# Round 1's first head of a hybrid trunk: two seven-product quads run product by product in turn

## The chip, the cores and the metric

The kernel runs on one core of one Trainium2 chip. Its engines are PE (TensorE), DVE (VectorE), ACT (ScalarE), POOL (GpSimd) and SP (SyncE, which issues nearly all DMAs). The metric is the time of one execution in microseconds (us), as the median of several runs. Times inside an execution are read from a profile of one of them.

## What is computed

One layer of a decoder trunk over 2048 tokens of width 1024, in fp32. Cut to what matters:

```python
hn = rms_norm(h, norm_g)
proj = jnp.einsum('bld,de->ble', hn, w_in)            # 1024 -> 8 * 512
cx, cb, cc, cg, q, k, v, rg = jnp.split(proj, 8, axis=-1)
conv_out = short_conv(cx, cb, cc) * silu(cg)
qf, kf = rotary(q, pos) * 128 ** -0.5, rotary(k, pos)
ret = head_group_norm(retention_chunkwise(qf, kf, v)) # 4 heads of 128, chunks of 128
mixed = concatenate([conv_out, ret * silu(rg)])
out = rms_norm(h + einsum('ble,ed->bld', mixed, w_out))
```

Nearly all matmul work is the projection by `w_in` and the one by `w_out`.

## The kernel before, in words

**Rounds, units, quads.** The tokens are done in two rounds of 1024. In each, four conv groups and four retention heads ("units") are run in a fixed order; each unit needs two "quads". A quad is a product of a 2 x 2 arrangement of weight blocks (for a head: keys and values by the lower and upper half of the 1024 inputs; then queries and gates) by a 2 x 2 arrangement of input blocks, with 512 tokens in each. It is done in one of two ways.

- `quad_plain` (line 293) multiplies all eight pairs of blocks. Its input operands are the blocks themselves, numbers 0, 1, 7 and 5.
- `quad` (line 236) does the same with seven products, in the Strassen-Winograd manner. Its input operands 0 to 6 are two blocks and five others (sums of blocks, and block 5); its weights are four blocks and three sums, which POOL forms in `stationary`. Three of the seven products are copied out of PSUM by ACT (line 243, `tc`), and DVE adds them to others. `take(i, j, bank, copy)` receives each result.

**Parts.** Every fp32 operand is split into a high part (ACT, line 112, or line 115 where the norm's gain is multiplied in) and a low part (DVE, line 113 or 116), and a product of two blocks is three matmuls (low by high, high by low, high by high) for each of four slices of 128 inputs: 12 matmuls of 128x512. High and low parts of weights are `wh` and `wl`, in rings of three buffers (RING); those of inputs `mh` and `ml`, one buffer for each operand and slice; number 7 has no buffer of its own and uses that of number 4. So an input operand of round 1 can be written once the last quad of round 0 has finished its product of that number.

**Sums.** The four sums of input blocks that round 1 needs are formed during round 0 by DVE (`prepare`), written to DRAM (`sums_x`) and read back by `prepared` (tiles `t`).

**The start of round 1.** `moving` loads the 16 blocks of `x` and splits them (operands 0, 1, 7, 5). Then the weights of the first quad are loaded and split as plain blocks, in buffers of operand 3. Head 0 runs keys and values with `quad_plain`: 96 matmuls. Two of the four sums are loaded and split ahead of it in the program, two behind it (`rest_of_sums`), and behind those the last conv group's result is stored. Queries and gates follow as a seven-product `quad`; in its steps the values and keys are taken to the other layout: `part` copies the 16-bit halves apart on ACT (line 677), a DMA transpose moves them (line 670), and `join` and `join_keys` copy them together again (lines 769 and 760). `weigh` scales the values (line 775). The state and score matmuls (lines 807 to 831) come after.

**Other work on DVE.** Keys and queries are rotated by `rotary`: two half operations (lines 658 and 659), a product and a sum (lines 660 and 661). Gates are multiplied by a row factor (line 750). POOL also does two products for the end of each conv group (line 596).

**The order of the rows.** Every engine takes its instructions in a fixed order. It is set at build time by a scheduler that goes by the program's order and by its own estimate of times; `issue_after` and priorities bend it. Where engines depend on each other, semaphores make them wait, and what is behind a waiting instruction on its engine waits too.

## Time and profile before

| | us |
|---|---|
| median of 3 runs | 869.21 (868.64 to 869.86) |
| the profiled execution's own time | 868.33 |
| its span, first to last instruction | 866.5 |
| PE busy | 855.4 (99%) |
| DVE busy | 725.7 (84%) |
| ACT busy | 497.8 (57%) |
| POOL busy | 394.6 (46%) |

The granted TensorE clock is 0.998 of full speed over the span. Round 1's first plain matmul starts at 360.70 us of the span.

In a timeline, a line gives start (us from the start of the span), duration, engine, line of the kernel, operation, result and operands with their shapes, and how many like it follow each other; in brackets stands the idle time of the engine just before it and what ended it. Operations overlap a little with the one before on their engine, and matmuls by half, so what an operation takes is read from the distance of two starts. In the lines of windows, each engine's busy time is followed by its number of instructions, and at the end stand the granted clock, the DMA engines' busy share and GB/s.

### The profile page before, as it was taken

Reading aid. Unit: us, or ns where it says so; the run is one execution under the profiler, and the core shown is the slowest. Engines: PE = TensorE matmul, PEld = TensorE weight load, DVE = VectorE, ACT = ScalarE, POOL = GpSimd, SP = SyncE. Lnnn points to the kernel's source line nnn. Section 1 sums busy time; section 2 is a strip of 40 time slices with the busy share of each in tenths; the row PEclk is TensorE's granted clock in tenths of the full one; section 3 lists DMA queues with packets and bytes.
Section 4 is the critical chain, followed back from the end, with each engine's and each line's share of the span. In section 5 each row is a group of like instructions: output and inputs, shape, how many; then the busy total and the mean of one; then the engine's idle time right before and its main releaser. Section 6 shows DMA issues by size and latency. Waiting matters only on the chain.

```text
span 866.5 us, 12699 instructions
## 1 busy us (share of the span) xinstructions
PE 855.4 (99%) x4216; PEld 705.1 (81%) x4216; DVE 725.7 (84%) x1194; ACT 497.8 (57%) x899; POOL 394.6 (46%) x286
## 2 busy tenths in 40 slices
PE   9999999999999999999999999999999999999996
PEld 6778888888787778788888888888888888788885
DVE  7899988888988977989789898988767799877663
ACT  8676548384755554948374757544333566545553
POOL 0662332423145554352242323354746555677773
PEclk9999999999999999999999999999999999999999
DMA  9724235454656633845264845646123584555431
GB/s 339 233 79 89 72 85 154 113 149 135 159 169 190 199 98 98 313 149 146 62 158 121 159 134 124 205 113 216 48 78 81 173 326 136 169 165 178 156 134 73
DMA packets 127218, 129.51 MB, mean 149 GB/s; under 512 B 58352, under 2 KB 75568, under 8 KB 127152
## 3 DMA queue, kind: packets, MB, share of 16 engines
q1 hardware_dynamic: 126576, 128.30, 50.0%
q8 instruction: 33, 0.54, 0.3%
q10 hardware_dynamic: 576, 0.40, 0.1%
q14 instruction: 33, 0.27, 0.1%
HBM read 90.91 MB, written 25.17 MB: 134 GB/s over the span
## 4 chain that ended last, share of the span: by engine, by line
PE 78%; DVE 6%; issue 1%; ACT 0%; POOL 0%; POOLq 0%; DVEq 0%
PE pj L236 66%; PE pj L293 5%; PE ms L831 1%; PE ms L820 1%; PE ms L830 1%; PE ms L807 1%; DVE wl L113 1%; PE ms L456 1%; DVE ml L113 1%; DVE ml L116 0%; DVE yo L121 0%; DVE yo L906 0%; DVE yo L941 0%; ACT n L407 0%; DVE tc L121 0%
## 5 line engine op out<-in xcount | busy, mean ns | idle before, releaser
L236 PE MATMUL pj<-mh,wl 128*128 128x512 f32 x1008 | 396.0, 393 | 1.3 <-DVE wl L113 0.7
L236 PE MATMUL pj<-mh,wh 128*128 128x512 f32 x1008 | 393.1, 390 | 0.0
L236 PE MATMUL pj<-ml,wh 128*128 128x512 f32 x1008 | 392.9, 390 | 0.0
L112 ACT CAST wh<-ra 128x512 fp32r<-128x512 f32 x216 | 133.9, 620 | 232.1 <-PE pj L236 193.6
L236 PEld LDWEIGHTS pj<-mh,wl 128*128 128x128 f32 x1008 | 189.3, 188 | 43.1 <-issue 1.5
L113 DVE TENSOR_TENSOR wl<-ra,wh 128x512 fp32r<-128x512 f32 x216 | 192.4, 893 | 36.6 <-ACT wh L112 35.2
L236 PEld LDWEIGHTS pj<-mh,wh 128*128 128x128 f32 x1008 | 189.3, 188 | 39.4
L236 PEld LDWEIGHTS pj<-ml,wh 128*128 128x128 f32 x1008 | 189.3, 188 | 38.1
L121 POOL TENSOR_TENSOR sa<-ra 128x512 f32<-128x512 f32 x36 | 54.1, 1504 | 108.8 <-DMA ra<-in_w_in 50.5
L124 POOL TENSOR_TENSOR ra<-sa,ra 128x512 f32<-128x512 f32 x36 | 51.3, 1424 | 81.8 <-DVE wl L113 79.6
L124 POOL TENSOR_TENSOR ra<-ra 128x512 f32<-128x512 f32 x36 | 59.1, 1641 | 59.2 <-PE ms L456 48.9
L151 POOL TENSOR_TENSOR ra<-ra 128x512 f32<-128x512 f32 x36 | 61.5, 1709 | 47.3 <-issue 35.2
L243 ACT COPY tc<-pj 128x512 f32<-128x512 f32 x108 | 62.6, 580 | 0.1
L293 PE MATMUL pj<-mh,mh 128*128 128x512 f32 x128 | 51.0, 401 | 0.6 <-ACT mh L115 0.6
L293 PE MATMUL pj<-mh,ml 128*128 128x512 f32 x128 | 50.0, 390 | 1.0 <-DVE ml L113 1.0
L293 PE MATMUL pj<-ml,mh 128*128 128x512 f32 x128 | 48.0, 391 | 0.0
L843 POOL TENSOR_TENSOR rp<-rs,neg_half 128x4 f32<-128x4 f32 x16 | 19.4, 1211 | 46.4 <-DVE rs L121 46.2
L596 POOL TENSOR_TENSOR c<-c,rr 128x512 f32<-128x512 f32 x14 | 25.7, 1834 | 22.2 <-DVE c L637 14.1
L906 DVE TENSOR_TENSOR yo<-pj,yo 128x512 f32<-128x512 f32 (+1 forms) x33 | 22.0, 671 | 15.9 <-PE pj L236 8.5
L917 POOL TENSOR_TENSOR z<-yo,final_g 128x512 f32<-128x512 f32 x16 | 26.8, 1674 | 18.6 <-DVE yo L906 18.6
L847 DVE TENSOR_SCALAR pm<-ms,mv,rp 128x128 f32<-128x128 f32 x64 | 21.9, 403 | 11.8 <-POOL rp L843 11.8
L112 ACT CAST wh<-sa 128x512 fp32r<-128x512 f32 x36 | 22.2, 618 | 16.0 <-PE pj L236 15.8
(153 smaller groups left out, 1223.2 us busy)
## 6 DMA issues: line engine op xcount, KB each, us to landing
ra<-in_w_in SPq DMA_DIRECT2D x126, 256.0 KB, 2.9
x<-in_xT SPq DMA_DIRECT2D x48, 256.0 KB, 5.0
w<-in_w_out SPq DMA_DIRECT2D x32, 256.0 KB, 4.7
ra<-mixed SPq DMA_DIRECT2D x32, 256.0 KB, 2.7
yo<-in_x SPq DMA_DIRECT2D x32, 256.0 KB, 4.6
ra<-in_x SPq DMA_DIRECT2D x16, 256.0 KB, 3.3
mixed<-c SPq DMA_DIRECT2D x16, 256.0 KB, 2.5
sums_x<-x SPq DMA_DIRECT2D x16, 256.0 KB, 2.8
```

The costliest lines, as they stand in the source:

```text
L112: nc.scalar.copy(out=hi, in_=src)
L113: lowered[0] = eng.tensor_tensor(out=lo, in0=src, in1=hi.bitcast(F32), op=ALU.subtract)
L121: eng.tensor_tensor(out=out, in0=a, in1=b, op=ALU.add)
L124: eng.tensor_tensor(out=out, in0=a, in1=b, op=ALU.subtract)
L151: summed[0] = nc.gpsimd.tensor_tensor(out=a12, in0=a12, in1=a11, op=ALU.subtract)
L236: nc.tensor.matmul(bank, a[:, ks], b, start=first and kt == 0 and n == 0, stop=kt == KH - 1 and n == 2, skip_group_check=not first,)
L243: copied[0] = nc.scalar.copy(out=c, in_=bank)
L293: nc.tensor.matmul(banks[i], a[:, ks], b, start=half + kt + n == 0, stop=half == 1 and kt == KH - 1 and n == 2,)
L596: eng.tensor_tensor(out=out, in0=a, in1=b, op=ALU.mult)
L847: nc.vector.tensor_scalar(out=y[:, cs], in0=o[:, cs], scalar1=mv[:, c, 0:1], scalar2=rp[:, c, :], op0=ALU.subtract, op1=ALU.mult,)
L906: last[0] = nc.vector.tensor_tensor(out=y[:, cs], in0=pp[:, cs], in1=y[:, cs], op=ALU.add)
L917: nc.gpsimd.tensor_tensor(out=ys[i][j], in0=y, in1=final_g[:, j * HB : (j + 1) * HB], op=ALU.mult)
```

## The change

Round 1's head 0 now runs both its quads as seven products, in turn: keys and values' product 0, queries and gates' product 0, keys and values' product 1, and so on. Four new functions replace `moving` and `quad_plain` there.

- `quads` runs the 14 products, with two PSUM banks for each quad, and takes results as `quad` does. Its `between` steps are called after each pair of products.
- `stationary_in_turn` gives a quad's weight parts one at a time, and forms its sums in the four buffers of the blocks themselves, with four POOL operations as before but no fifth buffer.
- `moving_in_turn` splits operands 0 and 1 ahead of the quads; the others follow as steps between the products: sums 2, 3, 4, block operand 5, sum 6.
- Operand 7, and with it four loads of `x` and four splits, is gone in round 1, and so are the four splits of plain weights; the seven splits of `stationary_in_turn` take their place.

In `head`, the keys are now split apart for the transpose after products 3 and 6, the values after products 5 and 6; the joins and weighing come behind the two quads. The store of the last conv group's result moves into the step of sum 6.

```diff
+    def stationary_in_turn(blocks):
+        a11, a12, a21, a22 = blocks
...
+        yield parts(a11)
+        add(nc.gpsimd, a21, a21, a22)
+        sub(nc.gpsimd, a11, a21, a11)
+        yield parts(a12)
+        sub(nc.gpsimd, a12, a12, a11)
+        yield parts(a11)
+        yield parts(a21)
+        sub(nc.gpsimd, a21, a22, a11)
+        yield parts(a21)
+        yield parts(a12)
+        yield parts(a22)
...
+        blocks(0, 0)
+        blocks(1, 0)
+        steps = [
+            lambda: sums(m, 1), lambda: sums(m, 0), lambda: sums(m, 2), lambda: blocks(1, 1), lambda: sums(m, 3),
+        ]
...
+    def quads(ws, m, takes, between=()):
...
+        for i in range(7):
+            for n, take in enumerate(takes):
+                if i < 2:
+                    banks[n][i] = ps_proj()
+                bank = banks[n][1 if i in (1, 3, 5) else 0]
+                product(n, i, bank, i in (0, 1, 3))
...
+            next(between, idle)()
...
-        quad(stationary(load_raw(w_loads(2 * h + 1))), m, take, (split_late, middle, late_middle))
-        with tc.issue_after(copied[0].ins):
+        if len(first) > 0:
+            steps = list(first) + [split_values, lambda: split_keys(1)]
+            steps[3] = lambda: (first[3](), split_keys(0))
+            ws = [stationary_in_turn(load_raw(w_loads(2 * h + n))) for n in range(2)]
+            quads(ws, m, (take_keys, take_queries), steps)
+            join_keys(0)
             join(1)
             weigh(1)
+            join(0)
+            weigh(0)
             join_keys(1)
+        else:
...
-            m, b = moving(load_x(r), gain_of)
-            first = [plain_parts(w_loads(0))]
+            m, first = moving_in_turn(load_x(r), gain_of, lambda m, n: prepared(m, sums_x, (n,)))
             load_tables()
-            prepared(m, sums_x, (1, 3))
-
-            def rest_of_sums():
-                prepared(m, sums_x, (0, 2))
+
+            def store_kept(last=first[4]):
+                last()
                 with tc.issue_after(loaded[0].ins):
                     kept.pop()()
```

How the rows move. The lines of the changed program are numbered anew (283 is the copy that was 243, 428 was 343, 743 to 746 were 658 to 661, 822 was 750).

First, ACT at the end of round 0, from the second of the two copies of the row factors on. Before:

```order
L343 ACTIVATE rr2_2924<-ms_3693 128x512
L112 CAST mh30_3904<-ra_3902 128x512
L115 ACTIVATE mh12_3844<-x_3842,gain_69 128x512
L112 CAST mh31_3916<-ra_3914 128x512
L115 ACTIVATE mh13_3850<-x_3848,gain_69 128x512
L112 CAST mh32_3910<-ra_3908 128x512
L112 CAST wh_3668<-ra_3637 128x512
L243 COPY tc_3759<-pj_3746 128x512
```

Now:

```order
L428 ACTIVATE rr2_2924<-ms_3693 128x512
L115 ACTIVATE mh12_3844<-x_3842,gain_69 128x512
L115 ACTIVATE mh13_3850<-x_3848,gain_69 128x512
L112 CAST wh_3668<-ra_3637 128x512
L283 COPY tc_3759<-pj_3746 128x512
L112 CAST mh20_3913<-t_3911 128x512
```

`pj_3746` is the bank of product 3 of round 0's last quad, into which its product 5 adds. The copy out of that bank has moved up by three rows. On PE, product 5 has moved up too: before, 25 plain matmuls of head 0 stood between products 4 and 5, now none.

Second, DVE at the fifth product of head 0's queries and gates. `wl_4179` was that product's low weight part, `wl_4183` the next one's:

```order
L113 TENSOR_TENSOR ml40_4124<-t_4121,mh40_4123 128x512
L113 TENSOR_TENSOR wl_4179<-ra_4153,wh_4178 128x512
L113 TENSOR_TENSOR ml41_4130<-t_4127,mh41_4129 128x512
L121 TENSOR_TENSOR qg_4222<-pj_4209,tc_4203 128x512
L113 TENSOR_TENSOR ml42_4136<-t_4133,mh42_4135 128x512
L113 TENSOR_TENSOR ml43_4142<-t_4139,mh43_4141 128x512
L658 TENSOR_TENSOR rot_4224<-qg_4222,rot_t_3805 64x512
L659 TENSOR_TENSOR rot_4224<-qg_4222,rot_t_3805 64x512
L113 TENSOR_TENSOR wl_4183<-ra_4151,wh_4182 128x512
```

Now `wl_4139` is the low part for the fifth product of keys and values, `wl_4158` that of queries and gates:

```order
L113 TENSOR_TENSOR wl_4139<-ra_3861,wh_4138 128x512
L113 TENSOR_TENSOR ml41_4058<-t_4055,mh41_4057 128x512
L113 TENSOR_TENSOR ml42_4064<-t_4061,mh42_4063 128x512
L113 TENSOR_TENSOR ml43_4070<-t_4067,mh43_4069 128x512
L116 SCALAR_TENSOR_TENSOR ml50_4112<-x_4109,gain_69,mh50_4111 128x512
L116 SCALAR_TENSOR_TENSOR ml51_4118<-x_4115,gain_69,mh51_4117 128x512
L116 SCALAR_TENSOR_TENSOR ml52_4124<-x_4121,gain_69,mh52_4123 128x512
L116 SCALAR_TENSOR_TENSOR ml53_4130<-x_4127,gain_69,mh53_4129 128x512
L113 TENSOR_TENSOR wl_4158<-ra_3869,wh_4157 128x512
```

The four splits of operand 5, which is used one pair of products later, have come in front of `wl_4158`.

Third, DVE where the next head begins: `wl_4427` and `wl_4431` were the low parts of its first two products, `wl_4411` and `wl_4415` are now. Before:

```order
L113 TENSOR_TENSOR wl_4427<-ra_4326,wh_4426 128x512
L121 TENSOR_TENSOR qg_4297<-pj_4249,tc_4241 128x512
L658 TENSOR_TENSOR rot_4299<-qg_4297,rot_t_3805 64x512
L659 TENSOR_TENSOR rot_4299<-qg_4297,rot_t_3805 64x512
L113 TENSOR_TENSOR wl_4431<-ra_4328,wh_4430 128x512
```

Now:

```order
L113 TENSOR_TENSOR wl_4411<-ra_4310,wh_4410 128x512
L746 TENSOR_TENSOR kv_4218<-kv_4218,rot_4220 128x512
L743 TENSOR_TENSOR rot_4243<-qg_4241,rot_t_3805 64x512
L744 TENSOR_TENSOR rot_4243<-qg_4241,rot_t_3805 64x512
L822 TENSOR_TENSOR qg_4288<-pj_3892,rr_2923 128x512
L745 TENSOR_TENSOR qg_4241<-qg_4241,rot_t_3805 128x512
L113 TENSOR_TENSOR wl_4415<-ra_4312,wh_4414 128x512
```

Five rows instead of three stand between the two, one of them (`qg_4288`) a product that reads the bank of the last product of queries and gates.

## The prediction

> **What bounds the kernel now.** I read the page's busy times and its chain first, then the windows around the start of round 1, then the timelines of PE, ACT, DVE and POOL there.

> ```profile
> PE   9999999999999999999999999999999999999996
> PE 78%; DVE 6%; issue 1%; ACT 0%; POOL 0%; POOLq 0%; DVEq 0%
> ```

> PE has work in every slice and carries the chain, so a matmul less is time less, and a wait of PE is time more, as long as nothing behind them takes it back. The change lies at 360 us, where round 0 ends. The windows there (PE busy, PEld, DVE, ACT, POOL, granted clock):

> ```profile
> 340.00:360.00 20.00, 20.00 (x89) 16.54 (x89) 18.43 (x29) 13.74 (x28) 9.22 (x8) 1.00 0.59 200
> 360.00:380.00 20.00, 18.97 (x84) 15.38 (x83) 19.92 (x27) 16.42 (x29) 6.80 (x4) 1.00 0.70 243
> 380.00:400.00 20.00, 20.00 (x90) 16.57 (x89) 17.62 (x29) 11.08 (x18) 6.48 (x2) 1.00 0.62 159
> ```

> At 360:380 DVE is busy for 19.92 of 20 us: in this stage it is the second engine at its limit. I call the products of round 0's last quad P0 to P6, those of the keys and values A0 to A6, of the queries and gates B0 to B6, and N0, N1 the next head's first two. PE's timeline:

> ```profile
> 360.48 0.39 PE L236 MATMUL pj<-mh,wh 128*128 128x512 f32 x1
> 360.70 0.39 PE L293 MATMUL pj<-mh,mh 128*128 128x512 f32 x1
> 362.12 0.50 PE L293 MATMUL pj<-mh,ml 128*128 128x512 f32 x1 [1.03 <-DVE ml L113]
> 367.46 0.39 PE L293 MATMUL pj<-ml,mh 128*128 128x512 f32 x1
> 367.69 0.39 PE L236 MATMUL pj<-mh,wl 128*128 128x512 f32 x1
> 372.90 0.39 PE L236 MATMUL pj<-mh,wh 128*128 128x512 f32 x1
> ```

> From 367.69 to 372.90 are 23 steps: 0.2265 us a matmul, 2.72 us a product of 12. P4 ends at 360.70; 25 plain matmuls (L293) stand between it and P5 at 367.69, and the second of them waits: 362.12 less 360.70 and one step is 1.19 us lost.

> **The change, part by part.** *Matmuls.* 96 become 84: 12 x 0.2265 = **-2.72 us**, all on PE's path.

> *P5's wait.* Now P5 follows P4 at once. It adds into the bank of P3, which ACT must have copied out, and that copy stands behind other work in ACT's row:

> ```profile
> 359.18 0.60 ACT L343 ACTIVATE rr<-ms 128x512 f32<-128x512 f32 x1
> 359.67 0.62 ACT L112 CAST mh<-ra 128x512 fp32r<-128x512 f32 x1
> 360.18 0.73 ACT L115 ACTIVATE mh<-x,gain 128x512 fp32r<-128x512 f32 x1
> 360.80 0.62 ACT L112 CAST mh<-ra 128x512 fp32r<-128x512 f32 x1
> 362.44 0.63 ACT L112 CAST wh<-ra 128x512 fp32r<-128x512 f32 x1
> 362.96 0.59 ACT L243 COPY tc<-pj 128x512 f32<-128x512 f32 x1
> ```

> Starts lie 0.62 apart behind an L115, 0.51 behind an L112. The order puts two L115, the cast and the copy behind L343: 359.67 + 2 x 0.62 + 0.51 = 361.42, the copy ends at 362.01, P5 starts some 0.05 later. PE loses 1.36 where it lost 1.19: **+0.17**. The plain matmuls that covered this copy are gone; the whole PE queue stands behind the wait. From there P6 is at 364.78, A0 at 367.50, each product 2.72 on, if nothing else waits: A4 at 389.26, B4 at 391.98.

> *DVE before B4.* Both quads now want all operands at once, where before the plain quad used 16 blocks and the sums had until the second quad. DVE's row order is fixed, so its path can be added up. Intervals, from these rows:

> ```profile
> 360.72 0.74 DVE L116 SCALAR_TENSOR_TENSOR ml<-x,gain,mh 128x512 fp32r<-128x512 f32 x1
> 361.38 0.68 DVE L113 TENSOR_TENSOR ml<-ra,mh 128x512 fp32r<-128x512 f32 x1
> 361.99 0.74 DVE L116 SCALAR_TENSOR_TENSOR ml<-x,gain,mh 128x512 fp32r<-128x512 f32 x1
> 377.64 0.69 DVE L658 TENSOR_TENSOR rot<-kv,rot_t 64x512 f32<-64x512 f32 x1
> 378.35 0.69 DVE L659 TENSOR_TENSOR rot<-kv,rot_t 64x512 f32<-64x512 f32 x1
> ```

> 0.66 from an L116 to the next, 0.60 from a plain operation, 0.71 from a half rotation. Up to 361.38 the order is that of before. Then 17 operations (2 of L116, 15 others) take 10.3: 371.7. The 18th, the keys' first sum, waits for A1's last matmul, 367.50 + 3 x 2.72 + 0.2 = 375.9, so DVE would stand for 4.2 us, with everything for A3 and later queued behind. From that sum up to the split of B4's low part are 27 (4 of L116, 4 half rotations, 19 others): 16.9 us, so 392.8. B4 is late by **0.9** even if GpSimd disturbs nothing.

> It does disturb. Beside POOL's rows stand DVE's:

> ```profile
> 367.58 3.12 DVE L116 SCALAR_TENSOR_TENSOR ml<-x,gain,mh 128x512 fp32r<-128x512 f32 x3
> 370.62 4.09 DVE L113 TENSOR_TENSOR ml<-t,mh 128x512 fp32r<-128x512 f32 x3
> 376.44 1.18 DVE L116 SCALAR_TENSOR_TENSOR ml<-x,gain,mh 128x512 fp32r<-128x512 f32 x1
> 382.86 1.89 DVE L113 TENSOR_TENSOR ml<-t,mh 128x512 fp32r<-128x512 f32 x3
> 367.74 1.74 POOL L596 TENSOR_TENSOR c<-c,rr 128x512 f32<-128x512 f32 x1 [8.09 <-DVE c L637]
> 370.04 1.81 POOL L121 TENSOR_TENSOR sa<-ra 128x512 f32<-128x512 f32 x1 [0.55 <-DMA ra<-in_w_in]
> 371.93 1.63 POOL L124 TENSOR_TENSOR ra<-ra 128x512 f32<-128x512 f32 x1
> 375.45 1.61 POOL L124 TENSOR_TENSOR ra<-sa,ra 128x512 f32<-128x512 f32 x1 [1.89 <-DVE wl L113]
> 383.08 5.23 POOL L151 TENSOR_TENSOR ra<-ra 128x512 f32<-128x512 f32 x1 [6.02 <-issue]
> 388.27 1.29 POOL L596 TENSOR_TENSOR c<-c,tc 128x512 f32<-128x512 f32 x1
> ```

> Three L116 undisturbed are 2.06, three L113 1.88 (1.89 at 382.86). Beside the four POOL operations from 367.74 to 375.45 they lose 1.06 + 2.21 + 0.44 = 3.71, **0.93 for each**; at most 1.1. The last two cost DVE nothing, but there the POOL operation itself took 5.23.

> Of nine POOL operations in the stretch, six fall before the keys' sum: 6 x 0.93 = 5.6, of which the 4.2 of standing cover all but 1.4 (if DVE never had that hole, all 5.6 would count). Three fall behind: 2.8. B4 is late by 0.9 + 1.4 + 2.8 = **+5.1**, part of it already at B0, A1 and A3. Ends: 0.9, and 0.9 + (6.6 - 4.2) + 3.3 = 6.6. I take 0.93, since the rows it comes from are this stretch's own.

> [...]

> *DVE before N1.* From B4's start T, DVE has three operations and then a gates sum that waits for B4's end, T + 2.9. From it to N1's low part are 20 (4 half rotations, 16 others): 12.4, plus 0.05 to PE: T + 15.4. PE wants N1 six products after T, at T + 16.3: 0.9 to spare. Three POOL operations of the next head's sums fall there: 2.8 - 0.9 = **+1.9**. Ends: 0 and 3.3 - 0.9 = 2.4. Behind it the order of every engine soon is that of before.

> *Costed at nothing.* Two more DVE operations net are in the counts. ACT has more casts but stands 11.08 of 20 us busy at 380:400. The banks: N0 takes A6's, copied out during B6. The joins of keys and values, now behind the quads, feed matmuls that PE reaches only four products after N0, 10.9 us; a transpose lands in

> ```profile
> ra<-in_w_in SPq DMA_DIRECT2D x126, 256.0 KB, 2.9
> tr<-pl SPq DMA_TRANSPOSE x32, 3.2
> ```

> 3.2 us and ACT's copies behind it take a few us. Without that cover each us would count.

> Sum: -2.72 + 0.17 + 5.1 + 1.9 = **+4.5 us**.

> **The rivals.**

> *DVE keeps up.* Place: DVE between A0 and B4. If POOL's operations fall where DVE stands, or cost it nothing as at 383 us, only the 0.9 stays and N1 is in time: -2.72 + 0.17 + 0.9 = -1.65, 867.6. It decides at B4's low part: done before 392.0 plus some 2.5, and the change no longer loses. For it: the 4.2 us hole. Against it: POOL's nine operations are 1.29 each and in line.

> *POOL is the late one.* As at 383.08, back-to-back DVE work holds POOL off; the differences that A2, B2, A4 and B4 are split from then come late, and DVE stands at the split until POOL (1.29), ACT's cast (0.62) and its own 0.68 are through: 2.6 a stop. One stop on the path before A4; then eight operations of DVE (5.0 us) lie between A4's low part and B4's, against one product of 2.72, so 2.3 more; and 1.9 at N1: -2.72 + 0.17 + 2.6 + 2.3 + 1.9 = +4.3; with two stops +6.9, 876.1.

> *The next head's weights come late.* On SP they are behind a transpose that waits for ACT's copy of the keys, the last four sums' loads, which wait for DVE, and two stores. I estimate their issue at some 396 (when DVE, at 392.8 plus part of the delay above, has split the blocks whose buffers those loads take), landing 2.9 later (the row above), 399; N0's cast is due at about 405. Should they slip by 8, 2 to 3 us come on top of the forecast: +7, 876.2.

> *It doesn't do what it says*: the order has 84 matmuls in place of 96, so this is out.

> **How the numbers follow.** The profiled execution is 868.33 us (span 866.5), the median of the runs 869.21, 0.88 above. 868.33 + 4.5 = 872.8 for a profiled execution, 873.7 against the median. A measurement of this kernel can tell about 0.2% (1.74 us) from no change: 867.5 and 870.9 are the limits. Chances: the forecast 0.55 (of it 0.05 within 0.2%, where both DVE terms come at half), DVE keeps up 0.22 (0.12 faster, 0.10 same), POOL late 0.15, weights late 0.08. Faster 0.12, same 0.15, slower 0.73. Range 867.6 to 876.3: from the first rival to two stops or late weights.

> **What would show it.** Right: a PE wait of about 1.4 us before P5 on ACT's copy, waits on DVE's low parts from B0 on with the largest at B4, over 2 us, one at N1 of about 2, 84 matmuls in the quads' line, and no DVE pause from 376 to B4. Wrong: PE without a wait between A0 and N1 (then 866.7 to 867.6), or a wait whose releaser is a DMA, ACT's transposed copies, or POOL.

## The result and the profile after

The changed kernel takes **877.2 us** (median of 4 runs, 875.49 to 878.53) against 868.98 (868.64 to 869.86) for the kernel before in the same session: ratio 1.0087, 95% interval 1.0075 to 1.01. It is slower, as forecast, but by 8.2 us and not by 4.5, and lies above the range. The profiled execution took 877.12 us, its span is 875.3.

The page's chain of the changed kernel:

```profile
PE 63%; DVE 13%; issue 4%; DMA 3%; ACT 2%; POOL 0%; SPq 0%; POOLq 0%; DVEq 0%; ACTq 0%
```

DVE had 6% of the chain, now 13%. The windows of the changed stage (length; busy PE, PEld, DVE, ACT, POOL; granted clock):

```profile
360.00:380.00 20.00, 18.78 (x79) 14.31 (x78) 20.00 (x24) 10.76 (x20) 12.64 (x7) 1.00 0.67 243
380.00:400.00 20.00, 16.12 (x67) 11.87 (x67) 19.85 (x27) 14.34 (x24) 5.15 (x4) 1.00 0.27 75
400.00:420.00 20.00, 18.11 (x79) 14.59 (x80) 18.37 (x25) 11.57 (x18) 6.53 (x4) 1.00 0.57 149
```

DVE is full for 40 us where before it was full for 20, and PE, which had 20.00 in 380:400, has 16.12. PE's timeline shows where it stood (L276 is the single quad, L324 the two in turn):

```profile
362.28 0.39 PE L276 MATMUL pj<-mh,wh 128*128 128x512 f32 x1
363.78 0.47 PE L276 MATMUL pj<-mh,wl 128*128 128x512 f32 x1 [1.11 <-DVE wl L113]
...
387.92 0.40 PE L324 MATMUL pj<-mh,wl 128*128 128x512 f32 x1
389.48 0.50 PE L324 MATMUL pj<-ml,wh 128*128 128x512 f32 x1 [1.17 <-DVE ml L113]
...
397.42 0.39 PE L324 MATMUL pj<-mh,wh 128*128 128x512 f32 x1
399.85 0.50 PE L324 MATMUL pj<-mh,wl 128*128 128x512 f32 x1 [2.04 <-DVE wl L113]
400.19 0.40 PE L324 MATMUL pj<-ml,wh 128*128 128x512 f32 x1
...
416.11 0.39 PE L276 MATMUL pj<-mh,wh 128*128 128x512 f32 x1
418.38 0.50 PE L276 MATMUL pj<-mh,wl 128*128 128x512 f32 x1 [1.89 <-DVE wl L113]
```

These are P5, A3, B4 and N1; each start less the one before and a step of 0.2265 is what was lost: 1.27, 1.33, **2.20**, **2.05**. The releaser of these four is a low part of DVE. The step behind a wait is longer too: 400.19 less 399.85 is 0.34, 0.11 more than a step.

What P5 and P6 waited for, ACT, DVE and PE side by side:

```profile
362.98 0.59 ACT L283 COPY tc<-pj 128x512 f32<-128x512 f32 x1
362.96 0.68 DVE L113 TENSOR_TENSOR wl<-ra,wh 128x512 fp32r<-128x512 f32 x1
366.15 0.67 DVE L121 TENSOR_TENSOR tc<-pj,tc 128x512 f32<-128x512 f32 x1
366.88 0.50 PE L276 MATMUL pj<-mh,wl 128*128 128x512 f32 x1
```

The copy that the forecast named for P5 ended at 363.57, P5's own low part at 363.64, 0.07 later. P6 adds into the bank of P4, which DVE's sum (`tc`, 366.15) had to read first; it ended at 366.82.

How much of the 8.2 us lies in this stage? The last matmul of P4 began at 360.48 before (its row is in the prediction) and begins at 362.28 now, 1.8 later, in code that is the same in both. At 450 us, where both orders agree again, a matmul is 7.68 later than its counterpart. The difference of the two spans, 8.8 (875.3 - 866.5), is in four pieces: 1.8 ahead of the stage, **5.87 in it** (forecast 4.5), 0.79 behind it in common code, 0.3 between the last matmul and the end of the span (7.90 against 7.61). The profiled executions differ by as much, 8.79 (877.12 - 868.33).

### The profile page after: what moved, and what is told of

The parts are those of the page before. It is cut to its first block, busy times and chain, and to the rows that moved or that the text cites. A ratio compares the mean times of both kernels' runs of the same rounds, so it can differ in the third digit from the quotient of the medians.

```text
span 875.3 us, 12664 instructions
## 1 busy us (share of the span) xinstructions
PE 857.5 (98%) x4204; PEld 703.3 (80%) x4204; DVE 730.5 (83%) x1196; ACT 497.7 (57%) x899; POOL 399.3 (46%) x290
## 2 busy tenths in 40 slices
PE   9999999999999999999999999999999999999996
## 4 chain that ended last, share of the span: by engine, by line
PE 63%; DVE 13%; issue 4%; DMA 3%; ACT 2%; POOL 0%; SPq 0%; POOLq 0%; DVEq 0%; ACTq 0%
PE pj L276 56%; DVE wl L113 3%; DVE ml L113 2%; PE ms L920 1%; PE ms L921 1%; PE ms L910 1%; DMA w<-in_w_out 1%; PE ms L897 1%; PE pj L324 1%; DVE qg L950 1%; DMA ra<-mixed 1%; DVE rot L744 1%; DVE rot L743 1%; PE ms L541 1%; DMA t<-sums_w 1%
## 5 line engine op out<-in xcount | busy, mean ns | idle before, releaser
L276 PE MATMUL pj<-mh,wl 128*128 128x512 f32 x980 | 385.5, 393 | 4.4 <-DVE wl L113 4.0
L276 PE MATMUL pj<-mh,wh 128*128 128x512 f32 x980 | 382.2, 390 | 0.0
L276 PE MATMUL pj<-ml,wh 128*128 128x512 f32 x980 | 382.1, 390 | 0.0
L112 ACT CAST wh<-ra 128x512 fp32r<-128x512 f32 x224 | 139.0, 621 | 236.9 <-PE pj L276 188.4
L113 DVE TENSOR_TENSOR wl<-ra,wh 128x512 fp32r<-128x512 f32 x224 | 200.2, 896 | 38.4 <-ACT wh L112 37.4
L276 PEld LDWEIGHTS pj<-mh,wl 128*128 128x128 f32 x980 | 184.0, 188 | 46.7 <-DVE wl L113 2.3
L276 PEld LDWEIGHTS pj<-mh,wh 128*128 128x128 f32 x980 | 184.0, 188 | 38.5
L276 PEld LDWEIGHTS pj<-ml,wh 128*128 128x128 f32 x980 | 184.1, 188 | 36.8
L121 POOL TENSOR_TENSOR sa<-ra 128x512 f32<-128x512 f32 x35 | 52.2, 1491 | 105.3 <-DMA ra<-in_w_in 37.7
L124 POOL TENSOR_TENSOR ra<-ra 128x512 f32<-128x512 f32 x41 | 66.6, 1627 | 66.0 <-PE ms L541 48.4
L124 POOL TENSOR_TENSOR ra<-sa,ra 128x512 f32<-128x512 f32 x35 | 50.2, 1434 | 90.5 <-DVE wl L113 88.4
L151 POOL TENSOR_TENSOR ra<-ra 128x512 f32<-128x512 f32 x35 | 56.3, 1608 | 44.5 <-issue 31.7
L378 PE MATMUL pj<-mh,mh 128*128 128x512 f32 x96 | 39.4, 412 | 0.7 <-ACT mh L1098 0.7
L378 PE MATMUL pj<-mh,ml 128*128 128x512 f32 x96 | 38.3, 399 | 0.2 <-DVE ml L113 0.2
L378 PE MATMUL pj<-ml,mh 128*128 128x512 f32 x96 | 36.0, 397 | 0.0
L996 DVE TENSOR_TENSOR yo<-pj,yo 128x512 f32<-128x512 f32 (+1 forms) x33 | 22.0, 671 | 16.6 <-PE pj L276 9.1
L681 POOL TENSOR_TENSOR c<-c,tc 128x512 f32<-128x512 f32 x14 | 24.5, 1753 | 16.8 <-ACT tc L707 15.3
L121 DVE TENSOR_TENSOR tc<-pj,tc 128x512 f32<-128x512 f32 x28 | 19.2, 685 | 14.3 <-PE pj L276 14.2
## 6 DMA issues: line engine op xcount, KB each, us to landing
ra<-in_w_in SPq DMA_DIRECT2D x126, 256.0 KB, 2.9
x<-in_xT SPq DMA_DIRECT2D x44, 256.0 KB, 4.9
w<-in_w_out SPq DMA_DIRECT2D x32, 256.0 KB, 5.0
ra<-mixed SPq DMA_DIRECT2D x32, 256.0 KB, 2.8
yo<-in_x SPq DMA_DIRECT2D x32, 256.0 KB, 4.6
ra<-in_x SPq DMA_DIRECT2D x16, 256.0 KB, 3.2
mixed<-c SPq DMA_DIRECT2D x16, 256.0 KB, 2.6
sums_x<-x SPq DMA_DIRECT2D x16, 256.0 KB, 2.6
```

The costliest lines, as they stand in the source:

```text
L112: nc.scalar.copy(out=hi, in_=src)
L113: lowered[0] = eng.tensor_tensor(out=lo, in0=src, in1=hi.bitcast(F32), op=ALU.subtract)
L121: eng.tensor_tensor(out=out, in0=a, in1=b, op=ALU.add)
L124: eng.tensor_tensor(out=out, in0=a, in1=b, op=ALU.subtract)
L151: summed[0] = nc.gpsimd.tensor_tensor(out=a12, in0=a12, in1=a11, op=ALU.subtract)
L276: nc.tensor.matmul(bank, a[:, ks], b, start=first and kt == 0 and n == 0, stop=kt == KH - 1 and n == 2, skip_group_check=not first,)
```

## The experiments

The theory: in this stage DVE is the bound, its row is full, and the order of that row and what GpSimd takes from it set PE's waits. The rivals: what comes late at B4 is something that DVE itself waits for; GpSimd costs DVE nothing; and, for the 1.8 that no term of the forecast held, that the start belongs to the program. All medians below are of one session's runs beside the kernel before, whose medians were 869.25, 869.5 and 869.01 in the three sessions.

| kernel | median us | ratio (95%) | P4's end to 450 us |
|---|---|---|---|
| changed, again | 876.68 | 1.0087 (1.0074 to 1.0101) | +7.78 |
| four splits later | 874.91 | 1.0066 (1.0053 to 1.0079) | +4.26 |
| no GpSimd sums | 872.23 | 1.0038 (1.0025 to 1.0051) | +2.86 |
| splits and rotations later | 871.94 | 1.0035 (1.0021 to 1.0049) | +1.54 |
| quads one after the other | 874.33 | 1.0056 (1.0043 to 1.0069) | +4.93 |
| eight unused matmuls | 876.97 | 1.0092 (1.0077 to 1.0108) | +7.15 |
| sums on VectorE | 875.2 | 1.0067 (1.0054 to 1.0079) | +5.63 |
| four splits and unused matmuls | 874.16 | 1.0058 (1.0046 to 1.007) | +3.97 |
| splits, rotations, sums | 871.69 | 1.0031 (1.0018 to 1.0043) | +0.97 |
| all, and next head's sums | 870.02 | 1.0012 (1.0004 to 1.0021) | +0.21 |

The last column is by how much more than at P4's end a matmul at 450 us is late against its counterpart in the kernel before, in the one profiled execution. Four of these executions hold a stretch of TensorE at half speed, of which more below: the first, that of no GpSimd sums, those of the unused matmuls alone and of the sums on VectorE.

**The two kernels again.** No edit.

> The changed kernel once more, unedited. In its first profile PE was 1.7 us later than the kernel before at 10 us, in code that is the same in both, and 5.6 later between P4 and the next head. Theory 'start by chance': the start moves from one execution to the next (0 to 2 us at 10 us), the stage's 5.6 stays within 0.5, and the time is 875 to 878. Rival 'the start belongs to the program': PE is again 1.5 to 1.9 us later at 10 us. Rival 'the stage itself varies': the pauses before B4 (2.2) and N1 (2.05) differ by more than 0.5 from the first profile.

> The kernel before once more, unedited, for a second profile of it. In five profiles of changed kernels that share their first 355 us with it, the 10th step of TensorE began between 8.3 and 10.5 us; in the first profile of the kernel before at 8.8. Theory (the start is by chance): again between 8.3 and 10.5, and no half-speed stretch of TensorE behind 12 us, since its longest wait there is 1.2 us. Rival (the start belongs to the program): 8.8 within 0.2.

The changed kernel: 876.68 us. The matmul ten behind that at 4.87 us (the 10th step) began at 8.33, against 8.78 in the first profile of the kernel before and 10.47 in that of the changed one; in the second profile of the kernel before it began at 9.30. In all profiles of this study it lies between 8.33 and 10.47: the start is by chance, and the first profile of the kernel before an early one. P4's end is 0.2 to 1.8 later than there in each of the others, the unedited kernel included (0.74).

The pauses were the same to 0.03 us (P5 1.27, A3 1.35, B4 2.21, N1 2.04), so they don't vary. One thing was new. PE behind N1 in this profile of the changed kernel:

```profile
415.34 0.39 PE L276 MATMUL pj<-mh,wh 128*128 128x512 f32 x1
417.61 0.50 PE L276 MATMUL pj<-mh,wl 128*128 128x512 f32 x1 [1.88 <-DVE wl L113]
417.94 0.39 PE L276 MATMUL pj<-ml,wh 128*128 128x512 f32 x1
418.17 0.39 PE L276 MATMUL pj<-mh,wh 128*128 128x512 f32 x1
418.40 0.58 PE L276 MATMUL pj<-mh,wl 128*128 128x512 f32 x1
418.77 0.63 PE L276 MATMUL pj<-ml,wh 128*128 128x512 f32 x1
419.20 0.63 PE L276 MATMUL pj<-mh,wh 128*128 128x512 f32 x1
...
422.05 0.40 PE L276 MATMUL pj<-mh,wl 128*128 128x512 f32 x1
```

Steps of 0.43 in place of 0.2265: from 418.17 to 422.05 are ten steps, 3.88 in place of 2.27, so 1.6 us lost. The granted clock was 0.61 in 418:420 and 0.53 in 420:422. That is most of the difference between +7.78 here and +5.87 in the first profile, which had no such stretch.

**Four splits behind B4's low part.**

```
             if i == 3:
                 for n, w in enumerate(ws):
                     ready[n].append(next(w))
                 with tc.issue_after(lowered[0].ins):
                     next(between, idle)()
```

> The changed kernel, but VectorE's four splits of the moving operand of product 5 come behind the split of B4's low part in VectorE's row, and product 4's two stationary operands are fetched ahead of them. Nothing is left out. Theory (VectorE's row is full from 357 to 403 us and its order alone sets when B4's low part is there): 4 x 0.6 us and the share of GpSimd's slow-down that falls on them move behind B4: the pause of 2.2 before B4 goes to under 0.4, A5 gains one of 0.5 to 1, N1's grows from 2.05 to 2.5 to 3.0; in all 0.7 to 1.3 us faster than the changed kernel. Rival (B4 waits for something that VectorE itself waits for: GpSimd's difference, a transfer): the pause before B4 stays at 2 and the time is within 0.4 of the changed kernel's.

PE at A5 and at N1 in that kernel (L325 is the two quads):

```profile
399.64 0.39 PE L325 MATMUL pj<-mh,wh 128*128 128x512 f32 x1
400.57 0.51 PE L325 MATMUL pj<-mh,wl 128*128 128x512 f32 x1 [0.54 <-DVE wl L113]
...
414.12 0.39 PE L276 MATMUL pj<-mh,wh 128*128 128x512 f32 x1
416.64 0.50 PE L276 MATMUL pj<-mh,wl 128*128 128x512 f32 x1 [2.14 <-DVE wl L113]
```

The wait before B4 is gone; A5 now waits 0.70, and N1's wait is 2.30 (2.5 to 3.0 was expected). The time falls by 1.8 us, 0.5 more than the theory's upper figure. In the changed kernel B4's low part waited for nothing but its place in DVE's row: by the order of the rows, POOL's last difference ended at 391.78 and ACT's cast for it at 395.63, while DVE, never idle there, came to the split at 399.12.

**No GpSimd sums in the two quads.** The eight sums and differences of weight blocks are left out, and the blocks themselves are split in their place.

```
-        add(nc.gpsimd, a21, a21, a22)
-        sub(nc.gpsimd, a11, a21, a11)
...
+        for a in (a11, a12, a11, a21, a21, a12, a22):
+            yield parts(a)
```

> The changed kernel without the eight GpSimd sums and differences of the weights' blocks in the two quads that run in turn: the blocks themselves are split in their place, so the seven products are made of other operands. As many VectorE operations and matmuls as in the changed kernel. Theory (each GpSimd operation with two inputs costs VectorE about 0.93 us while its row is full): the pauses before P5 to A4 nearly go, B4's falls from 2.2 to about 1, N1's stays near 2 since what remains of GpSimd's work lies there; 3 to 4.5 us faster than the changed kernel, so near the kernel before. Rival (GpSimd costs VectorE nothing and the row alone is too long): within 0.5 of the changed kernel. Rival (GpSimd itself is the late one): the same gain, but in the changed kernel's trace VectorE would then have to stand idle at the splits, which it did not, so I give that little.

872.23 us, 4.4 less than the changed kernel. DVE in this kernel up to the keys' first sum (kv, 376.68) and at B4's low part (393.29):

```profile
372.37 1.14 DVE L113 TENSOR_TENSOR wl<-ra,wh 128x512 fp32r<-128x512 f32 x1 [0.57 <-ACT wh L112]
375.15 0.69 DVE L113 TENSOR_TENSOR wl<-ra,wh 128x512 fp32r<-128x512 f32 x1 [1.64 <-ACT wh L112]
376.68 0.69 DVE L121 TENSOR_TENSOR kv<-pj,tc 128x512 f32<-128x512 f32 x1 [0.83 <-PE pj L315]
...
393.29 0.68 DVE L113 TENSOR_TENSOR wl<-ra,wh 128x512 fp32r<-128x512 f32 x1
```

Here is the standing time that the prediction put ahead of the keys' sum: 0.57 + 1.64 + 0.83 = 3.04 us (forecast 4.2 with no GpSimd work at all; two GpSimd operations are left in this stretch). In the changed kernel there is none; its DVE at the same place, and GpSimd's rows beside it:

```profile
372.06 1.78 DVE L681 TENSOR_TENSOR tc<-tc,rr 128x512 f32<-128x512 f32 x1
373.76 0.68 DVE L722 TENSOR_TENSOR c<-pj,c 128x512 f32<-128x512 f32 x1
374.36 4.58 DVE L113 TENSOR_TENSOR wl<-ra,wh 128x512 fp32r<-128x512 f32 x3
378.87 0.68 DVE L121 TENSOR_TENSOR kv<-pj,tc 128x512 f32<-128x512 f32 x1
...
399.12 0.68 DVE L113 TENSOR_TENSOR wl<-ra,wh 128x512 fp32r<-128x512 f32 x1
```

```profile
369.18 2.41 POOL L121 TENSOR_TENSOR ra<-ra 128x512 f32<-128x512 f32 x1 [7.36 <-DMA ra<-in_w_in]
371.54 1.75 POOL L681 TENSOR_TENSOR c<-c,rr 128x512 f32<-128x512 f32 x1
373.25 3.45 POOL L124 TENSOR_TENSOR ra<-ra 128x512 f32<-128x512 f32 x2
376.66 1.74 POOL L681 TENSOR_TENSOR c<-c,tc 128x512 f32<-128x512 f32 x1
378.36 3.44 POOL L124 TENSOR_TENSOR ra<-ra 128x512 f32<-128x512 f32 x2
```

Three splits took 4.58 where three alone take 1.88. From P5's start to B4's low part are 399.12 - 363.78 = 35.34 us with the sums and 393.29 - 362.70 = 30.59 without: 4.75 more, and the 3.04 of standing filled: 7.79 for eight sums, **0.97 each** (forecast 0.93). (One of the eight ran ahead of P5, at 353.13; without it DVE is 1.08 us further on in its row when P5 starts, so the count holds its price too.) P5's wait, which was expected nearly to go, stays at 1.31; B4's falls to 1.23. N1's stays at 2.09, since GpSimd's work there is that of the next head.

**Splits and rotations later.** The edit of the four splits, and

```
         def turn_held():
             with tc.issue_after(lowered[0].ins):
                 for d in held_back:
                     rotary(d, tables[0])
...
-            steps[3] = lambda: (first[3](), split_keys(0))
+            steps[4] = lambda: (turn_held(), first[4](), split_keys(0))
```

with the first halves' rotations of keys and queries collected in `held_back`.

> The edit of the run before with four splits moved behind B4's low part, and also the eight half rotations of the first halves of keys and queries held back until B4's low part is split, with the keys' first planes behind them. Nothing is left out. Theory (VectorE's row order): with 8 x 0.7 us more out of the way ahead of B4, no pause before B4; the products behind it are short, N0 and N1 wait 2 to 3 us between them; 3 to 4.5 us faster than the changed kernel, so about 1 us slower than the kernel before, more by what the start costs. Rival (the work only moves and comes due at N1, since VectorE's total up to N1 is too long): N1's pause grows by what B4's shrinks, and the time is within 1 us of the changed kernel's.

871.94 us, 4.7 less than the changed kernel (expected: 3 to 4.5). No wait before B4, N0 or N1 (2 to 3 us between the last two were expected); A5 waits 1.05, and the fifth of the next head's products 1.55, on ACT's copy. So most of the held work is hidden, not moved to N1.

**The quads one after the other.** Only the two loops are exchanged.

```
-        for i in range(7):
-            for n, take in enumerate(takes):
+        for n, take in enumerate(takes):
+            for i in range(7):
```

> The changed kernel with its two quads one after the other in place of product by product in turn; both still in seven products, nothing left out. VectorE's operations are the same, the moving operands of A3 to A6 are wanted twice as early, and behind A6 no more are wanted. Theory (VectorE's row is the bound, so PE waits wherever demand runs ahead of it): the waits move into A1 to A5, 5 to 7 us in all with none before the queries' products or N1, and since VectorE catches up during the queries' products the time is 0.5 to 2 us below the changed kernel's. Rival (turn-taking is what keeps the waits small): 1 us or more slower than the changed kernel. Either way slower than the kernel before by 4 to 9 us.

PE in that kernel, from A2 to A5:

```profile
375.98 0.47 PE L324 MATMUL pj<-mh,wl 128*128 128x512 f32 x1 [1.43 <-DVE wl L113]
...
380.13 0.50 PE L324 MATMUL pj<-mh,wl 128*128 128x512 f32 x1 [1.18 <-ACT mh L112]
382.13 0.50 PE L324 MATMUL pj<-ml,wh 128*128 128x512 f32 x1 [1.50 <-DVE ml L113]
...
384.54 0.50 PE L324 MATMUL pj<-ml,wh 128*128 128x512 f32 x1 [0.52 <-DVE ml L113]
...
390.07 0.50 PE L324 MATMUL pj<-ml,wh 128*128 128x512 f32 x1 [0.63 <-DVE ml L116]
```

As the theory had it, the waits stand where demand runs ahead of DVE (idle 1.43, 1.18, 1.50, 0.52 and 0.63 us) and none is left from B0 to N1. By the ratios, 1.0056 and 1.0087, it is 2.7 us faster than the changed kernel, 0.7 more than expected. Turning between the quads doesn't make the waits smaller.

**The sums on VectorE.** `nc.gpsimd` becomes `nc.vector` in the four lines of sums and differences; the same work.

> The changed kernel with the eight sums and differences of the two quads' stationary blocks on VectorE in place of GpSimd; nothing left out. Theory (each GpSimd operation with two inputs takes 0.93 us from a VectorE that is always busy, while the same operation in VectorE's own row takes 0.60): VectorE's work up to B4 shrinks by 8 x 0.33 = 2.6 us, of which some comes back since the sums now stand ahead of A0's splits (1.3 there): 0.5 to 2 us faster than the changed kernel, the pauses at A3 gone. Rival (GpSimd's share costs VectorE less than 0.6 each, or GpSimd's lateness was the cause): 8 x 0.60 = 4.8 us more in VectorE's row, 2 to 5 us slower than the changed kernel.

By the ratios 1.7 us less than the changed kernel, as the theory had it; A3's wait of 1.33 is gone, B4's stays at 2.16. The same window of the changed kernel, and then of this one:

```profile
360.00:403.00 43.00, 37.90 (x158) 28.65 (x157) 41.55 (x53) 25.19 (x45) 17.79 (x10) 1.00 0.51 172
```

```profile
360.00:403.00 43.00, 39.65 (x169) 30.91 (x168) 41.50 (x62) 26.61 (x47) 7.79 (x5) 1.00 0.51 168
```

DVE got through 62 operations in the time in which it got through 53. Half of GpSimd's load (17.79 to 7.79) was paid by DVE at more than the price of doing it itself.

**The clock behind long waits.** Eight matmuls that nothing uses, ahead of N1's first:

```
+        if kept_warm[0]:
+            kept_warm[0] = False
+            for _ in range(8):
+                nc.tensor.matmul(yb, w[0][0][:, :P], m[0][0][0], start=True, stop=True, skip_group_check=True)
```

> The changed kernel with eight matmuls of N0's operands into N1's bank ahead of N1's first (which starts the bank anew), 1.8 us of work that nothing uses, where PE waits 2.05 us. In two of five profiles TensorE ran at half speed for some 3 us just behind the wait before N1 and lost 1.6 to 1.8 us by it. Theory (a wait of some 2 us sometimes brings the clock down): with PE busy through it no fall behind N1, the wait there 0.2 to 0.5, the time 0.3 to 1.5 us below the changed kernel's, and the mean granted clock of its runs nearer to 0.998 than to 0.996. Rival (the wait costs its own length and no more, the falls have another cause): within 0.3 us of the changed kernel, with falls in that place as before.

876.97 us: no gain, so the expected time was missed. There was no slow stretch behind N1, but one behind B4, whose wait was as long as ever:

```profile
396.17 0.39 PE L330 MATMUL pj<-mh,wh 128*128 128x512 f32 x1
398.56 0.50 PE L330 MATMUL pj<-mh,wl 128*128 128x512 f32 x1 [2.00 <-DVE wl L113]
...
399.39 0.63 PE L330 MATMUL pj<-mh,wl 128*128 128x512 f32 x1
399.82 0.63 PE L330 MATMUL pj<-ml,wh 128*128 128x512 f32 x1
```

The runs' clocks were 0.996, 0.995, 0.996 and 0.996. So both waits had to go at once: the four splits moved, and the unused matmuls.

> The edit that moved four splits behind B4's low part (its profile's longest waits: 1.35 at A3, 0.70 at A5, 2.30 at N1) together with the eight unused matmuls ahead of N1's first. No wait of 2 us is then left: N1's is 0.4 to 0.9 behind 1.8 of unused work. Theory (half-speed stretches follow waits of some 2 us or more): none behind 12 us, every run's mean granted clock 0.997 or above, and a time 0 to 0.8 us below that of the four splits alone, where two of five runs had 0.994 and 0.997. Rival (they fall anywhere in this stage): clocks of 0.996 and less as often as there, and the same time or longer.

N1's wait in this kernel, the rows of L300 being the unused work:

```profile
413.47 1.98 PE L300 MATMUL pj<-mh,wh 128*128 128x512 f32 x8
415.74 0.50 PE L278 MATMUL pj<-mh,wl 128*128 128x512 f32 x1 [0.29 <-DVE wl L113]
```

PE comes to N1's real work no earlier, yet the time is 0.7 us below that of the four splits alone (ratios 1.0058 and 1.0066), the clocks are 0.998 four times and 0.997 once, and no stretch at half speed is left behind 12 us. All as the theory had it, though the two intervals overlap, and a run's mean clock is a weak witness: a fall of 3.4 us moves it by 0.002, but every profile also ends with 2.9 to 5.2 us at half speed behind its last matmul, which by itself moves it by 0.001.

Why do the falls come behind some waits of 2 us and not behind others? In the record of the granted clock that each of the thirteen profiles holds, the stretches between the first rise and the last fall are whole multiples of 3.413 us (860.16 us at full speed, 252 of them, in the first profile of the changed kernel; 121, 1 and 132 of them in its second), and each fall lasts one. So in these profiles the clock changed on a grid of this step. Here are steps of that grid around N1's wait (length; busy PE, PEld, DVE, ACT, POOL; granted clock), two of the second profile of the changed kernel, then one of its first:

```profile
415.04:418.45 3.41, 1.53 (x8) 0.94 (x7) 3.38 (x6) 3.41 (x5) 0.77 (x1) 1.00 0.70 131
418.45:421.86 3.41, 3.41 (x10) 2.67 (x9) 2.00 (x2) 2.81 (x6) 0.85 (x1) 0.50 0.26 65
```

```profile
416.53:419.95 3.42, 1.56 (x7) 1.30 (x8) 3.42 (x5) 3.42 (x6) 1.49 (x1) 1.00 0.58 115
```

The wait of 2.04 us in the second profile lies whole in one step, and the next step ran at half speed; that of 2.05 in the first is cut by the grid into 0.19 and 1.85, and no fall followed. (PE's busy times, 1.53 and 1.56, are nearer to each other than the waits, since the modelled ends of matmuls count in them.) Counted over all profiles, from the first rise to the last matmul, the steps ahead of the four falls hold 2.09 to 2.28 us of waits (longer steps behind them included), and no other step holds more than 1.96. What goes with the falls in these profiles is the sum within a step: with the quads one after the other, waits of 1.34 and 1.77 us stand 0.22 apart, and in its profile the grid parts them into steps of 1.78 and 1.80.

**Towards a version that beats both.** The splits and rotations later, with the sums on VectorE; then the keys' rotation moved up behind A4's low part, and the next head's four sums on VectorE too:

```
-            with tc.issue_after(lowered[0].ins):
-                for d in held_back:
+            for d, mark in zip(held_back, marks):
+                with tc.issue_after(mark.ins):
...
+        eng = nc.vector if on_vector[0] else nc.gpsimd
```

> The changed kernel with three edits together: the four splits and the first halves' rotations behind B4's low part, and the two quads' eight sums on VectorE. Nothing left out. Theory (the gains add, since all shorten or empty the same VectorE row): the first two gave 5 us and the sums 1.7; with 0.3 to 1.7 more here it is 870.2 to 871.7, 0.5 to 2 us slower than the kernel before, since P5's wait stays and one near 1 us is left before the queries' sixth product. Rival (with the splits moved VectorE has room already and the sums in its own row only cost): 872 to 874.

> The edit of the run before, with the keys' held rotation placed behind the split of A4's low part (those of the queries stay behind B4's), and the next head's first four sums of stationary blocks on VectorE too. Nothing left out. Theory (VectorE's row): the wait at the next head's products shrinks from 1 to 1.5 us to under 1; 0 to 1 us below the run before, and so between 0.5 us faster and 1.5 us slower than the kernel before: at best a draw, since 2.7 us of matmuls saved stand against P6, A0, the queries' sixth product and the next head. Rival (GpSimd at the next head costs nothing): the same as the run before, or up to 1 us slower.

871.69 and 870.02 us (one execution of the first, of 4925.39 us, is left out of its ratio). The first is at the upper end of what was expected; its fifth product of the next head still waits 1.57. By the ratios the second is 1.7 us below it, where 0 to 1 was expected. Its waits are three: P5 1.08, A5 1.54, N2 1.03. From P4's end to 450 us its waits and longer steps are 4.4 us of PE's time, against 1.7 in the kernel before; the 2.7 between them are what the 12 matmuls save, and steps longer by a few ns make the 0.21 of the table. The kernel before still wins by 0.04 to 0.21%: moving DVE's work about brings the change back to a draw, no further.

## Why the prediction was right in direction and too small

*Matmuls, -2.72.* 4204 matmul records against 4216: right.

*P5, +0.17.* P5's wait is 1.27 and a longer step of 0.08 behind it, against 1.19 and 0.11 before: +0.05. ACT's copy ended 1.29 behind the start of P4's last matmul (forecast 1.53), but the last to come was P5's own low part, 0.07 later, which had no term; in seven of the nine edited kernels the releaser is the copy. So the path through ACT holds, and that the low part came no later is luck. P6 waits too, 0.27 and 0.11, for the DVE sum that reads its bank: +0.43 in all. P6 had no term.

*DVE before B4, +5.1: the mechanism is shown, and the size nearly.* A0 to B4 lost 5.6 us in the first profile, 4.8 in waits and 0.8 in the longer steps behind them; the largest wait is at B4 (2.20), with smaller ones at A1 and A3 as forecast, and one at A0 in place of B0. The parts hold one by one: 0.97 for each GpSimd sum (0.93); 3.04 us of standing once the sums are gone (4.2, less two GpSimd operations that stay); 16.6 us from the keys' sum to B4's low part without the sums (16.9); nine GpSimd operations, five of them ahead of the keys' sum and four behind, where I had six and three. "DVE keeps up" is out: there is standing time only without the sums. "POOL is the late one" is out: by it DVE would stand at the splits, and in the changed kernel it never stands from P5 to B4; and the same sums on VectorE cost less. "The next head's weights come late" is out too: N1 waits for DVE's split, which began at 417.65, when by the order of the rows ACT's cast for it had ended at 414.86.

*DVE before N1, +1.9.* 2.05 and 0.11 behind it; three GpSimd operations lie there, as counted.

Not in the sum at all was the longer step behind each wait: 0.08 to 0.11 each, ten times, about 1 us.

*The step that failed* is the sum, "-2.72 + 0.17 + 5.1 + 1.9 = +4.5 us", and the line that adds it to the time, "868.33 + 4.5 = 872.8 for a profiled execution, 873.7 against the median". It prices each wait of PE at its length, puts what follows a wait at nothing, and takes the stage for the whole difference. In the stage the change cost 5.87, 1.4 more than forecast: 0.4 at P6, 0.9 in the longer steps from A0 to N1, 0.4 in steps that are longer by a few ns up to 450 us, while the waits that had terms came to 0.3 less than forecast. In the profiled executions 1.8 more came from the start, which the second profiles showed to be chance; but the medians are no nearer. What fills most of the rest is a cost that no term and no rival named: behind four of the nine waits of 2.04 to 2.30 us TensorE ran at half speed for 3.4 us. The mean granted clock of the runs is 0.998 over 38 of the kernel before and 0.9969 over 8 of the changed one; 0.0011 of 875 us is about 1 us, an estimate. With 5.87 of the stage and the 0.3 at the end it makes 7.2 of the 7.8 between all runs' medians (877.04 and 869.2). The last 0.6 is within what the starts scatter by, and I can't assign it; nor have I found why the end is longer (behind the last matmul's start 7.61 in both profiles of the kernel before, 7.90 to 8.36 in all eleven of changed ones), and the 0.79 behind the stage in the first profile was not there in the second (8.52 late at 450 us, 8.51 at the end).

## What to carry to other kernels

When a second engine is close to its limit (DVE was busy for 19.92 of 20 us before), halving the lead time of its work can cost more than the saved matmuls bring, as here (a stage 5.87 us longer with 2.72 us of matmuls saved); add up its row up to each due time, with what GpSimd takes from it, and move what isn't due. An operation that GpSimd takes over from a full VectorE can cost it more than doing it would, as here (0.97 us against 0.60). Price a wait of PE above its length: here the step behind it took 0.31 to 0.34 us in place of 0.2265, and where waits came to 2.09 us or more within a step of 3.413 us of the clock's record, half speed followed for one such step.
